# Expert 14's weighted rows added in memory like the others'; only the last expert is placed by TensorE in the combination

## The chip, the cores and the metric

The kernel runs on one core of one Trainium2 chip. A core has TensorE for matrix products (PE in the profile), VectorE (DVE), ScalarE (ACT), GpSimd (POOL) and SyncE (SP), each with its own list of instructions that it works through in order, and 16 DMA engines that move data between the chip's large memory and the on-chip memories. SyncE issues most of the transfers; GpSimd issues those that gather or scatter rows by an index. Engines wait for each other on semaphores. The metric is device time in microseconds of one execution, the median of several.

## The reference, cut to what matters

The program is a trunk of two layers over 512 tokens of width 1024. Each layer has a token mixer and then a mixture of 16 gated experts, of which each token uses two. What this case is about is the end of a layer:

```python
x = _layernorm(DEEPNORM_ALPHA * x + mix, ln1_g[l], ln1_b[l])
ffn = _hier_moe(x, ...)                      # sum over a token's two experts, weighted
x = _layernorm(DEEPNORM_ALPHA * x + ffn, ln2_g[l], ln2_b[l])

# inside _hier_moe, for all experts e:
h = silu(x @ w_gate[e]) * (x @ w_up[e]) * combine[..., e]
return einsum('bsef,efd->bsd', h, w_down)
```

The kernel divides by ALPHA ahead of a norm, so that it adds the experts' rows to x itself; the norm's epsilon is divided to match.

## The kernel before, in words

The 512 tokens stand as four tiles of 128 rows. After the first norm of a layer the four tiles are written twice to memory: to `x1d`, from which the experts gather their tokens, and to `acc`, to which the experts add their results (`keep`, line 1807). An expert has a block of up to 96 tokens. Its steps (class `Expert`) are: a selection matrix of 0 and 1 (`hot`), the row numbers from it (`index`), a gather of the rows from `x1d` (line 1446, GpSimd), transposes and a split of each operand into a high and a low part so that products keep float32's precision (`x`, `split`), the gate and up products (`up`), the activation (`act`), transposes of the hidden block (`hidden`) and the down product in two parts (`down`).

What then happens to the 96 result rows depends on the expert. For experts 0 to 13, `out` lets ScalarE scale them by the token's weight into a tile in two halves, and GpSimd issues one DMA that adds the 96 rows to the rows of `acc` that the index names (line 1598, a scatter with addition). For experts 14 and 15 nothing goes to memory. `place_t` turns the expert's selection matrix round by four small matmuls and a copy by ScalarE (`oht`), `y` leaves the scaled rows on the chip as a high part (ScalarE) and a low part (VectorE), and in the combination TensorE multiplies the turned selection with them, which places the rows in the tile's 128 rows.

The order of an expert's steps is written out (`ORDER`, line 59; loop at line 1962), with steps of neighbouring experts between each other; the results of expert e-1 leave within the turn of expert e, so those of expert 14 in the turn of expert 15. The loop pins the order of all but the last two turns, and a scheduler orders the rest by its own costs.

Behind the experts stands a loop for tokens beyond 96 of an expert (lines 1983 to 2039). Its count is read from a tile by every engine. With this case's inputs the count is 0 and the body is skipped, but the program counts semaphores as if it had run: on the skipping path each engine raises its own count by the number of the body's instructions, and GpSimd raises the counts of the body's DMAs, with one instruction behind waits for all counts of earlier software DMAs (`INC_SWDGE_SEM` in the profile, an `ISA` row in the order).

Then comes the combination (from line 2041). `load_x(acc)` loads the four tiles of `acc`; the combination's steps stand in `COMB0` for the first layer and `COMB1` for the second. For tile i, `F` is the first group of matmuls into two banks, `p` places the last expert's rows on top, `a` takes the sum out of the banks, `s`, `g`, `v`, `f` are the second norm. For tile 0 (`ACCD`) VectorE adds the banks to the loaded rows; for tiles 1 to 3 the loaded rows are added by TensorE, by a float32 product with the identity matrix ("identity matmul" below), and ScalarE takes the sum out together with its row sums. In the first layer the steps `w0` to `w3` split the first input weights of the next layer between them, and the transposes of the finished tiles open the next layer; in the second layer the finished tiles go to the output.

Of the kernel before, what the change touches and what calls it, by code (L numbers as in the profile page):

```python
# [25 lines left out]
E = 16  # L26
# [15 lines left out]
ACCD = (0,)  # L42
FL = 3
BLK = 96
# [142 lines left out]
class Buf:  # L187
# [4 lines left out]
    def free(self):  # L192
        assert self.live
        self.live = False
        self.pool.put(self)
# [17 lines left out]
def tile_trunk(ctx: ExitStack, tc: tile.TileContext, ins, out, dbg=None, depth=DEPTH):  # L213
# [22 lines left out]
    V, A, G, T = Pinned(nc.vector, "V"), Pinned(nc.scalar, "A"), nc.gpsimd, Pinned(nc.tensor, "T")  # L236
# [119 lines left out]
    ident = const.tile([128, 128], F32, name="ident")  # L356
# [202 lines left out]
    for l in range(depth):  # L559
# [1042 lines left out]
        def make(e):  # L1602
            def load_gu(t, q):
                load(t, ins["w_gu"], ((l * E + e) * 4 + q) * 128 * 1024, [[1024, 128], [1, 1024]])

            def load_dn(t, f):
                load(t, ins["expert_w_down"], ((l * E + e) * FE + f * 128) * D, [[D, 128], [1, D]])

            return Expert(load_gu, load_dn, e >= E - 2, e, e == 0)

        ex = [make(e) for e in range(E)]
# [18 lines left out]
        xr = load_x(ins["x"] if l == 0 else x2d)  # L1630
# [59 lines left out]
        for a, q in enumerate(order):  # L1690
            w = wo_split(raws[0][a], a)
# [124 lines left out]
        for c in WSEQ.split():  # L1816
            if c[0] == "Z":
                i = int(c[1])
# [21 lines left out]
            t = tiles[int(c[1])]  # L1840
# [14 lines left out]
        for _ in range(NU):  # L1855
            m, n = todo.pop(0)
# [61 lines left out]
        def all_experts():  # L1918
# [14 lines left out]
            for e in range(E):  # L1933
                if e == HE:
                    held[0] = None
                pin[0] = PIN0 <= e < E - PIN1
                a = ex[e]
                b, c, d = (ex[e + n] if e + n < E else None for n in (1, 2, RA))
                z = ex[e - 1] if e else None
                steps = {  # L1940
                    "act": a.act,
                    "out": (z.out if e < E - 1 else z.y) if z else None,
                    "hid": a.hidden,
                    "d0": lambda: a.down(0), "d1": lambda: a.down(1),
                    "sd0": lambda: a.split(4), "sd1": lambda: a.split(5),
                    "place": a.place_t if e >= E - 2 else None,
                }
                if e == E - 1:
                    steps["d0"] = steps["d1"] = None
# [26 lines left out]
        with tc.issue_after(kins.ins), tc.issue_after(tiles[NT - 1].cp.ins):  # L1976
            (first_w, first_w2), fr, fr2 = all_experts()
# [6 lines left out]
        with tc.If(rv > 0), tc.For_i(0, rv, 1):  # L1984
# [43 lines left out]
            m = Expert(load_gu, load_dn)  # L2028
# [13 lines left out]

        ln2 = load_ln(2)
        xr = load_x(acc)
        last = ex[E - 2:]

        def place(pz, i, m, first=False, final=False):
            t = m.oht[:BLK, i * 128:(i + 1) * 128]
            for hf, p in enumerate(pz):
                w = slice(hf * 512, hf * 512 + 512)  # L2050
                T.matmul(p.ap, t, m.yh[:BLK, w], start=first, stop=False, skip_group_check=True)
                T.matmul(p.ap, t, m.yl[:BLK, w], start=False, stop=final, skip_group_check=True)

        def first_places(i):
            pz = [(P4 if i > 1 else P5).get() for _ in range(2)]
            place(pz, i, last[0], first=True)
            if i not in ACCD:
                for hf, p in enumerate(pz):
                    T.matmul(p.ap, ident, xr[i][:, hf * 512:hf * 512 + 512], start=False, stop=False,
                             skip_group_check=True)  # L2060
            return pz

        class Norm:

# [8 lines left out]
            def place(self):  # L2073
                if self.pz is None:
                    self.first()
                place(self.pz, self.i, last[1], final=True)

            def sum(self):
                z = xr[self.i]
# [62 lines left out]
                first_w2[i] = (first_w2[i] or []) + win_split(fr2[i][q:q + 1], 0, 256, True)  # L2142
                free(fr2[i][q])

        last[1].down(0)
        last[1].down(1)
        norms = [Norm(i) for i in range(NT)]
        steps = {"y": last[1].y}
        for i in range(NT):
            n = norms[i]  # L2150
            for c, f in (("F", n.first), ("p", n.place), ("a", n.sum), ("s", n.square), ("g", n.scale),
# [3 lines left out]
            pin[0] = CPIN and c not in ("y", "w0", "w1", "w2", "w3")  # L2155
            steps[c]()
        pin[0] = False
        for m in last:
            free(m.oht, m.yh, m.yl)
        for n in range(NS, NS + KD):  # L2160
            pool.whole.remove(n)
        free(ln2)
# [67 lines left out]
```

## Time and profile before

| what | value |
|---|---|
| three runs | 1066.09, 1066.67, 1069.11 us; median 1066.67 |
| profiled execution | 1070.26 us, its span 1067.8 us |
| TensorE's granted clock, mean | 0.974 |
| busy share PE / DVE / ACT / POOL | 93% / 78% / 60% / 25% |
| scatters with addition | 28, 14 per layer |

The span is the time from the first to the last instruction; a share is the busy time over it. The first layer's combination lies at about 512 to 545 us, the second layer's at about 1040 to 1068 us, the end of the program. Times in all views are counted from the span's start.

### The profile page before, as it was taken

How to read it: one execution, taken by the hardware profiler on the slowest of the kernel's cores; microseconds unless marked ns; L12 is line 12 of the kernel's file. 1: busy time of each engine (PE TensorE's matmuls, PEld its weight loads, DVE VectorE, ACT ScalarE, POOL GpSimd, SP SyncE). 2: the span in 40 equal slices, each digit the busy share in tenths (PEclk: the TensorE clock that was granted, in tenths of full speed). 3: DMA queues.
4: the chain of work that ended last, by engine and by line, in shares of the span. 5: the costliest groups of instructions: out<-in, count | busy, mean ns of one | idle time of the engine just before them, and what ended most of it. 6: DMA issues, size and time to landing. Idle time of an engine off the chain costs nothing. (4 is left out here: it accounts for less than half of the span.)

```text
span 1067.8 us, 15553 instructions
## 1 busy us (share of the span) xinstructions
PE 996.5 (93%) x5310; PEld 739.2 (69%) x5310; DVE 836.0 (78%) x1832; ACT 644.6 (60%) x1182; POOL 267.2 (25%) x232
## 2 busy tenths in 40 slices
PE   6999999988998999999999999999799989999995
PEld 6876788555687666666598768876466876666653
DVE  8995557787749799999969955577876498999996
ACT  5565646555524588888646564466464347778874
POOL 1000002223003255565100000022220123556652
PEclk9999989998999899999999998999999989999998
DMA  7211100132656889996532120011347477999933
GB/s 305 69 45 45 40 21 21 35 126 99 234 198 218 282 288 345 335 324 213 204 139 70 40 69 1 21 40 41 118 138 246 168 275 264 311 339 337 308 94 155
DMA packets 51795, 176.76 MB, mean 166 GB/s; under 512 B 8169, under 2 KB 8681, under 8 KB 51712
## 3 DMA queue, kind: packets, MB, share of 16 engines
q1 hardware_dynamic: 45216, 160.42, 42.2%
q0 software_dynamic: 6496, 15.31, 6.0%
q8 instruction: 42, 0.69, 0.3%
q14 instruction: 41, 0.34, 0.1%
HBM read 159.61 MB, written 23.59 MB: 172 GB/s over the span
## 5 line engine op out<-in xcount | busy, mean ns | idle before, releaser
L230 PE MATMUL b<-xt,s 128*128 128x512 f32 (+3 forms) x1484 | 327.1, 367 | 13.8 <-ACT s L230 8.6
L230 PE MATMUL b<-s,s 128*128 128x512 f32 (+7 forms) x1308 | 324.7, 404 | 14.0 <-ACT s L230 7.1
L230 PEld LDWEIGHTS b<-xt,s 128*128 128x128 f32 (+2 forms) x1484 | 234.0, 183 | 80.3 <-issue 11.5
L230 DVE TENSOR_TENSOR s<-s,s 128x1024 fp32r<-128x1024 f32 (+8 forms) x254 | 247.6, 1000 | 50.5 <-ACT s L230 41.7
L230 PEld LDWEIGHTS b<-s,s 128*128 128x128 f32 (+3 forms) x1308 | 185.0, 173 | 99.7 <-DVE s L230 22.6
L230 ACT ACTIVATE s<-b 128x512 f32<-128x512 f32 (+8 forms) x282 | 135.0, 496 | 191.2 <-PE b L230 182.3
L230 ACT ACTIVATE s<-s 128x1024 fp32r<-128x1024 f32 (+5 forms) x219 | 191.6, 910 | 85.1 <-DVE s L230 31.8
L230 PE MATMUL b<-s,xt 128*128 128x256 f32 (+2 forms) x944 | 209.1, 362 | 0.4 <-POOL s L1523 0.4
L230 PEld LDWEIGHTS b<-s,xt 128*128 128x128 f32 (+1 forms) x944 | 150.6, 192 | 34.7 <-issue 4.8
L230 DVE TENSOR_TENSOR xt<-s,xt 128x1024 fp32r<-128x1024 f32 (+1 forms) x106 | 118.3, 1122 | 13.8 <-ACT xt L230 13.7
L230 ACT ACTIVATE xt<-s 128x1024 fp32r<-128x1024 f32 (+1 forms) x107 | 110.4, 1042 | 26.1 <-PE b L230 17.7
L230 PE MATMUL b<-ident,s 128*128 128x128 f32 (+3 forms) x736 | 107.4, 273 | 18.6 <-POOL s L1338 7.7
L230 PEld LDWEIGHTS b<-ident,s 128*128 128x128 f32 (+3 forms) x736 | 81.5, 153 | 53.3 <-ACT s L230 13.9
L1598 POOL DMA_INDIRECT acc<-s,slx x28 | 55.3, 1976 | 99.3 <-ACT s L230 79.4
L230 ACT ACTIVATE s<-b,mx,qsc 128x512 f32<-128x512 f32 x64 | 49.7, 782 | 25.5 <-DVE mx L230 25.1
L1338 POOL TENSOR_SCALAR s<-s,sums 128x512 f32<-128x512 f32 x48 | 37.6, 788 | 105.7 <-DVE sums L230 93.6
L1094 POOL MEMSET s<- 128x780 f32 x4 | 3.0, 756 | 219.9 <-DVE s L230 186.3
L230 DVE TENSOR_REDUCE mx<-b 128x1 f32<-128x512 f32 x64 | 43.2, 686 | 18.3 <-PE b L230 17.9
L1446 POOL DMA_INDIRECT s<-x1d,slx x30 | 40.5, 1351 | 57.4 <-PE b L230 23.0
L230 DVE TENSOR_TENSOR s<-b,s 128x192 fp32r<-128x192 f32 (+3 forms) x92 | 46.9, 524 | 4.6 <-POOL s L1127 2.6
L230 PE MATMUL b<-xt 128*96 128x512 f32 x160 | 48.0, 406 | 1.4 <-DVE xt L230 1.4
L230 ACT ACTIVATE s<-b,slw 96x512 f32<-96x512 f32 (+1 forms) x60 | 39.1, 682 | 14.9 <-PE b L230 8.3
(254 smaller groups left out, 983.9 us busy)
## 6 DMA issues: line engine op xcount, KB each, us to landing
s<-in_w_gu_dram SPq DMA_DIRECT2D x128, 512.0 KB
s<-in_expert_w_down_dram SPq DMA_DIRECT2D x64, 512.0 KB
s<-in_w_inp_dram SPq DMA_DIRECT2D x36, 512.0 KB
s<-in_w_outp_dram SPq DMA_DIRECT2D x16, 512.0 KB
x1d<-s SPq DMA_DIRECT2D x8, 512.0 KB
acc<-s SPq DMA_DIRECT2D x8, 512.0 KB
s<-acc SPq DMA_DIRECT2D x8, 512.0 KB
s<-in_x_t_dram SPq DMA_DIRECT2D x4, 512.0 KB
```

Source lines behind the costliest of these rows:

```text
L230: r = f(*a, **kw)
L1094: G.memset(cb.ap, 0.0)
L1338: (V if hd in NORMV else G).tensor_scalar(P.ap, P.ap, sums, 0.0, op0=OP.mult, op1=OP.add)
L1446: self.ga = G.indirect_dma_start(out=self.xg[:BLK], out_offset=None, in_=x1d[0:128 * n, :], in_offset=bass.IndirectOffsetOnAxis(ap=ix[:BLK ...
L1598: G.indirect_dma_start(out=acc[:, :], out_offset=bass.IndirectOffsetOnAxis(ap=self.ix[:BLK, 0:1], axis=0), in_=yt[:BLK], in_offset=None, b ...
```

## The change

Expert 14 now leaves like experts 0 to 13: ScalarE scales its rows into a tile, and GpSimd adds them to `acc` by a scatter, in the turn of expert 15. Its `place_t` and `y` are gone, and with them its part of the combination. `F` keeps only the identity matmuls (none for tile 0), and `p` places expert 15's rows alone.

```diff
-                    "out": (z.out if e < E - 1 else z.y) if z else None,
+                    "out": z.out if z else None,
...
-                    "place": a.place_t if e >= E - 2 else None,
+                    "place": a.place_t if e == E - 1 else None,
...
-        last = ex[E - 2:]
-
-        def place(pz, i, m, first=False, final=False):
-            t = m.oht[:BLK, i * 128:(i + 1) * 128]
+        last = ex[E - 1]
+
+        def first_places(i):
+            pz = [(P4 if i > 1 else P5).get() for _ in range(2)]
+            if i not in ACCD:
+                for hf, p in enumerate(pz):
+                    T.matmul(p.ap, ident, xr[i][:, hf * 512:hf * 512 + 512], start=True, stop=False,
+                             skip_group_check=True)
+            return pz
+
+        def place(pz, i):
+            t = last.oht[:BLK, i * 128:(i + 1) * 128]
             for hf, p in enumerate(pz):
                 w = slice(hf * 512, hf * 512 + 512)
-                T.matmul(p.ap, t, m.yh[:BLK, w], start=first, stop=False, skip_group_check=True)
-                T.matmul(p.ap, t, m.yl[:BLK, w], start=False, stop=final, skip_group_check=True)
-
-        def first_places(i):
-            pz = [(P4 if i > 1 else P5).get() for _ in range(2)]
-            place(pz, i, last[0], first=True)
-            if i not in ACCD:
-                for hf, p in enumerate(pz):
-                    T.matmul(p.ap, ident, xr[i][:, hf * 512:hf * 512 + 512], start=False, stop=False,
-                             skip_group_check=True)
-            return pz
+                T.matmul(p.ap, t, last.yh[:BLK, w], start=i in ACCD, stop=False, skip_group_check=True)
+                T.matmul(p.ap, t, last.yl[:BLK, w], start=False, stop=True, skip_group_check=True)
...
-                place(self.pz, self.i, last[1], final=True)
+                place(self.pz, self.i)
...
-        last[1].down(0)
-        last[1].down(1)
+        last.down(0)
+        last.down(1)
...
-        steps = {"y": last[1].y}
+        steps = {"y": last.y}
```

On GpSimd, in the first layer, this is what stands behind expert 13's scatter and ahead of the loop's count (`nblk`), before; `xt` and `s` are buffers, `slx` the row numbers, and the brackets name the semaphores waited for (`DMASW` those of GpSimd's own DMAs):

```order
L1598 DMA acc<-s_677_4794,slx_4404 512x1024 [waits DMASW4_49,DMASW3_49,Activation_49]
L1523 TENSOR_TENSOR xt<-s_621_4467,xt 128x512 [waits DVE_49,DMAHW5_49,PE_49,Activation_49]
L1523 TENSOR_TENSOR xt<-s_605_4371,xt 128x512 [waits DVE_49,DMAHW1_49,PE_49,Activation_49]
L1523 TENSOR_TENSOR xt<-s_625_4481,xt 128x512 [waits DMAHW7_49,Activation_49,Pool_49]
L1983 TENSOR_LOAD nblk_3194 [waits DVE_49]
L1984 COMPARE_AND_BRANCH x2
```

And the same place of the changed kernel, with the semaphore instruction of a path around the loop's body as its last row:

```order
L1598 DMA acc<-s_677_4794,slx_4404 512x1024 [waits DMASW4_49,DMASW3_49,Activation_49]
L1523 TENSOR_TENSOR xt<-s_621_4467,xt 128x512 [waits DVE_49,DMAHW5_49,PE_49,Activation_49]
L1523 TENSOR_TENSOR xt<-s_605_4371,xt 128x512 [waits DVE_49,DMAHW1_49,PE_49,Activation_49]
L1523 TENSOR_TENSOR xt<-s_625_4481,xt 128x512 [waits DMAHW7_49,Activation_49,Pool_49]
L1598 DMA acc<-s_679_4839,slx_4512 512x1024 [waits DMASW4_49,Activation_49]
L1983 TENSOR_LOAD nblk_3194 [waits DVE_49]
L1984 COMPARE_AND_BRANCH x2
L1984 ISA [waits DMASW4_49,DMASW5_49,DMASW3_49,DMASW6_49,DMASW2_49,DMASW7_49,DMASW1_49,DMASW0_49]
```

The new scatter stands between the last weight split and the loop, ahead of the instruction that waits for all eight counts. On SyncE, behind the loop, the first load of `acc` waits for the software DMA count 5 in the changed kernel, where it was count 4; in both it is the value that the count has after the loop:

```order
L277 DMA s_724_5067<-acc 128x1024 [waits DMASW5_49,DMAHW7_49,DVE_49,PE_49]
L277 DMA s_725_5069<-acc 128x1024 [waits DMAHW0_49,Activation_49]
L277 DMA s_726_5071<-acc 128x1024 [waits DMAHW1_49,DVE_49]
L277 DMA s_727_5073<-acc 128x1024 [waits DMAHW2_49,DVE_49,Pool_49]
L277 DMA s_785_5600<-in_w_inp_dram 128x1024 [waits DMAHW3_49,Activation_49]
```

On ScalarE, in the first layer's combination, before: `s_742` to `s_750` and `s_789` are splits of the next layer's input weights, `xt<-b` are the high parts of expert 15's rows, `s_725` is the sum of tile 1 taken out of its banks.

```order
L230 ACTIVATE s_742_5152<-s_673_4772 128x1024
L230 ACTIVATE s_744_5156<-s_674_4774 128x1024
L230 ACTIVATE xt<-b_72,slw_4622 96x512
L230 ACTIVATE xt<-b_71,slw_4622 96x512
L230 ACTIVATE s_748_5182<-s_675_4776 128x1024
L230 ACTIVATE s_750_5186<-s_676_4778 128x1024
L230 ACTIVATE s_725_5073,ac_5121<-b_75 128x512
L230 ACTIVATE s_725_5073,ac_5121<-b_73 128x512
L230 ACTIVATE s_789_5628<-s_785_5620 128x1024
```

And of the changed kernel:

```order
L230 ACTIVATE s_742_5140<-s_673_4772 128x1024
L230 ACTIVATE s_744_5144<-s_674_4774 128x1024
L230 ACTIVATE xt<-b_71,slw_4622 96x512
L230 ACTIVATE s_748_5166<-s_675_4776 128x1024
L230 ACTIVATE s_750_5170<-s_676_4778 128x1024
L230 ACTIVATE s_789_5608<-s_785_5600 128x1024
L230 ACTIVATE s_725_5069,ac_5109<-b_74 128x512
L230 ACTIVATE s_725_5069,ac_5109<-b_75 128x512
```

One half of expert 15's rows has moved ahead of the loop, and the split of `s_785`, which the load behind the four of `acc` brings, has moved ahead of tile 1's sum.

## Rows read from the trace of the kernel before

**Rows 1.** Chain that ended last, 1036 to 1068 us: start, length, engine and tile.
```profile
1040.85 11.27 PE b L230 x40
...
1062.11 1.28 DVE s L230
```

**Rows 2.** TensorE's groups by shape, 1042.9 to 1057 us: expert 14's placement.
```profile
L230 PE MATMUL b<-s,s 96*128 96x512 f32 x16 | 4.4, 396 | 0.0
```

**Rows 3.** Scatters of line 1598: who waited, all landings; landing in 500 to 512 us.
```profile
  POOL acc L1598: 3.9, 1
...
DMA to landing us min/median/max: 5.6/8.9/10.3
...
DMA to landing us min/median/max: 5.6/5.6/5.6
```

**Rows 4.** Time line, first combination: start, length, instruction, [idle before <-what ended it].
```profile
504.62 1.43 POOL L1598 DMA_INDIRECT acc<-s,slx  x1 [2.26 <-DVE xt L230]
...
510.60 0.33 SPq L277 DMA_DIRECT2D s<-in_ln_g_dram  x1
510.71 1.52 POOL L1523 TENSOR_TENSOR xt<-s,xt 128x512 fp32r<-128x512 f32 x1 [1.45 <-DVE s L230]
...
511.53 1.38 ACT L230 ACTIVATE s<-b,slw 96x512 fp32r<-96x512 f32 x2 [0.31 <-PE b L230]
512.56 3.50 SPq L277 DMA_DIRECT2D s<-acc  x4
...
520.15 1.98 PE L230 MATMUL b<-s,ident 128*128 128x512 f32 x4 [0.65 <-DMA s<-acc]
...
523.63 0.60 ACT L230 ACTIVATE s<-b 128x512 f32<-128x512 f32 x1 [3.31 <-PE b L230]
...
524.78 1.06 ACT L230 ACTIVATE s<-s 128x1024 fp32r<-128x1024 f32 x1
...
537.87 7.87 PE L230 MATMUL b<-xt,s 128*128 128x256 f32 x65
...
545.47 1.34 PEld L230 LDWEIGHTS b<-ident,s 128*128 128x128 f32 x12
```

**Rows 5.** Queue records of the skipped loop on GpSimd, ns, first and second layer.
```profile
L1984 POOLq INC_SWDGE_SEM  x1: 756/756/756, 511.8 to 511.8; - x1
...
L1984 POOLq INC_SWDGE_SEM  x1: 1322/1322/1322, 1038.5 to 1038.5; - x1
```

**Rows 6.** Time line, second combination.
```profile
1028.09 1.39 ACT L230 ACTIVATE s<-b,slw 96x512 f32<-96x512 f32 x2 [0.64 <-PE b L230]
...
1029.76 1.78 POOL L1598 DMA_INDIRECT acc<-s,slx  x1 [1.75 <-ACT s L230]
...
1037.37 1.79 POOL L1523 TENSOR_TENSOR xt<-s,xt 128x512 fp32r<-128x512 f32 x1 [3.27 <-ACT xt L230]
...
1038.27 1.38 ACT L230 ACTIVATE s<-b,slw 96x512 fp32r<-96x512 f32 x2 [0.32 <-PE b L230]
...
1039.92 1.84 SPq L277 DMA_DIRECT2D s<-acc  x4
...
1046.24 1.88 PE L230 MATMUL b<-s,ident 128*128 128x512 f32 x4
...
1048.62 0.60 ACT L230 ACTIVATE s<-b 128x512 f32<-128x512 f32 x1 [0.56 <-PE b L230]
```

**Rows 7.** Busy time by engine (us), PEclk, DMA share and GB/s, one full microsecond.
```profile
1042.00:1043.00 1.00, 1.00 (x6) 0.67 (x5) 0.00 (x0) 0.29 (x1) 0.00 (x0) 1.00 1.08 414
```

**Rows 8.** The same view: length, PE, PEld, DVE, ACT, POOL busy, then PEclk, DMA.
```profile
762.70:769.50 6.80, 2.30 (x10) 1.39 (x9) 5.37 (x15) 5.45 (x10) 2.01 (x2) 1.00 0.29 98
769.50:776.30 6.80, 5.31 (x15) 2.92 (x16) 5.52 (x13) 2.62 (x4) 2.68 (x3) 0.50 0.00 0
865.20:872.00 6.80, 4.18 (x41) 3.87 (x40) 6.51 (x27) 4.24 (x7) 2.67 (x2) 1.00 0.53 167
872.00:878.80 6.80, 6.67 (x28) 5.80 (x29) 5.24 (x24) 2.54 (x5) 1.47 (x2) 0.50 0.95 324
```

More of the change, by code (lines that the diff above doesn't have):

```diff
@@ L2157, in tile_trunk @@
         pin[0] = False
-        for m in last:
-            free(m.oht, m.yh, m.yl)
+        free(last.oht, last.yh, last.yl)
         for n in range(NS, NS + KD):
```

## The prediction, as put on record

> **What bounds the kernel now.** I read the views in this order: the chain that ended last, the time line of the two combinations, the queue records of the loop behind the experts, the scatters, and the granted clock of stretches. In the second combination the chain runs through TensorE for 11.27 us, and then through VectorE and ScalarE to the last normalisation at 1062.11 us [rows 1]. TensorE is what the placement loads: 16 matmuls of expert 14's rows take 4.4 us there [rows 2], four of them per tile in front of that tile's identity matmul. So a look at the busy share alone says that the change takes work off the chain. What decides is another chain, that ends just ahead of the combination: the last scatter, GpSimd's semaphore instruction behind the skipped loop, the four loads of `acc`, the first identity matmul.
>
> In the kernel before, that other chain has room. The scatter of expert 13 leaves GpSimd at 504.62 us in the first layer and its data are in memory 5.6 us later, at 510.2 [rows 3, 4]; GpSimd raises the counts of the loop's DMAs from 511.8 to 512.56 [rows 5], and SyncE starts the loads of `acc` at 512.56 [rows 4]. So it was GpSimd's arrival at the loop that released the loads, not the scatter. In the second layer the same instruction runs from 1038.5 to 1039.82 [rows 5], and the loads start at 1039.92 [rows 6], though expert 13's scatter had left at 1029.76. The first layer's combination already waits a little for the loads: TensorE's first identity matmul has 0.65 us of idle time ended by the DMA of `acc` [rows 4]. In the second layer it starts at 1046.24 with no such wait [rows 6].
>
> **What the change removes.** Per layer: 4 matmuls that transpose expert 14's selection, ScalarE's copy of it, VectorE's two residues of 14's rows (ScalarE's two scalings stay, they only write elsewhere), and the 16 placement matmuls [rows 2]. The first three stand ahead of the loop, where the chain to come starts at ScalarE's scalings, which wait for the weight splits of the last experts and not for these; I cost them at nothing, at most 0.5 us gained per layer. The placement matmuls were at most 4.4 us per layer [rows 2]. They are no gain while TensorE waits for `acc` longer than it worked on them.
>
> **What it adds: one scatter, ahead of the loads.** Its source is ready when ScalarE's second scaling ends. First layer: 511.53 + 1.38 = 512.91 [rows 4]; second: 1038.27 + 1.38 = 1039.65 [rows 6]. GpSimd starts 0.28 us behind (1028.09 + 1.39 = 1029.48, the scatter at 1029.76) [rows 6]; its own split before it is over by then (512.23 and 1039.16) [rows 4, 6]. So the scatters start at 513.19 and 1039.93. From start to landed I take 5.6 us, the one scatter with nothing issued behind it; all scatters with a landing in the trace lie between 5.6 and 10.3, median 8.9 [rows 3], but those run beside weight loads. Landed: 518.8 and 1045.5.
>
> GpSimd then stands at the loop: the order shows that its semaphore instruction waits for every DMA count, the new scatter's too, and the first load of `acc` waits for a count that this instruction raises. It takes 0.76 to 1.32 us [rows 5], 1.04 in the middle, and SyncE follows 0.1 later. Loads of `acc`: 519.9 instead of 512.56, and 1046.7 instead of 1039.92, some 7 us late. Behind the waiting load on SyncE stand the other three and the input weights of the next layer; behind GpSimd's instruction nothing that is due. ScalarE's second weight split in the first layer waits for a raised count as well, and expert 15's second half stands behind it; that is over by 522, ahead of the rows of `acc`.
>
> From the first load to TensorE's first identity matmul (tile 1): 520.15 - 512.56 = 7.6 us in the first layer [rows 4], with the two 0.5 MB loads of the norm's gain and bias in front; at the 414 GB/s of a full stretch [rows 7] they take 2.5 us, which leaves about 5.0. The second layer bounds it by 1046.24 - 1039.92 = 6.3 [rows 6]. With 5.0: 524.9 and 1051.7, which is 4.8 and 5.5 us late.
>
> **Second layer.** All later steps follow tile 1's rows, and from tile 1 on the chain is VectorE's and ScalarE's, which the change leaves alone [rows 1]. So +5.5, and the clock: TensorE now stands idle some 7 us before the identity matmul. In the rows, after it worked 2.30 us of a 6.8 us stretch the next one was granted 0.50, after 4.18 us as well, from 1.00 before each [rows 8]; that is 1.2 in place of 2.4 GHz. From the identity matmul to tile 1's sum on ScalarE were 2.38 us (1046.24 to 1048.62) [rows 6], so at half speed all through it is 2.4 more; the low level may end midway, and I take 1.6. Sum +7.1.
>
> A page speaks against the change here. The Trainium skill, "TensorE: Matmul & The Clock Gate", section "What's actually happening", has it that the throttled state is the default and that activity releases it. The rows above agree with it. Without that rule the second layer would stand at +5.5 and the sum below 1.6 lower.
>
> **First layer.** The order puts the split of the first loaded input weight ahead of tile 1's sum on ScalarE; before it stood behind. Its load is the fifth in the queue. Three loads after tile 1's rows at 1.27 us each (0.52 MB at 414 GB/s) it is there at 528.7, and 1.06 us of split [rows 4] end at 529.8. TensorE alone would let tile 1's sum begin at 524.9 + 3.48 (523.63 - 520.15) [rows 4] = 528.4, at the low clock some 1.6 later, 530.0. Both say 530: tile 1's sum moves from 523.63 to 530.0, +6.4. VectorE's scaling of tile 0 stands behind tile 1's mean, and tile 0's and 1's transposes feed the next layer. Slack is not to be seen behind it: VectorE is through with tile 3 just as TensorE comes to its transposes at 545.47 [rows 4].
>
> **Sum.** 6.4 + 7.1 = 13.5 us. The profiled execution took 1070.26 us, 2.5 of it outside its span of 1067.8, and becomes 1083.8. It was 3.6 us above the median of the runs, 1066.67; so the median goes to 1080.2. Bounds: low, the semaphore instruction takes 0.76, tile 1's rows come 4.4 us after the issue (the middle between the 6.3 above and the 2.5 that two tiles need at 414 GB/s), and the clock stays: +4.6 in the second layer and, with the weight split, +5.3 in the first, 9.9 together. High, the scatter lands after 8.9: 3.3 more in each layer.
>
> **Rivals.**
> 1. The clock stays at 1.00 and the next layer's weights are there in time: 4.8 + 5.5 = +10.3, 1077.0. For it: the rows of the clock show what went before, not how much idle time it takes; against it: 7 us idle is more than the 4.5 of [rows 8]. Chance 0.2.
> 2. The scatter needs what most need, 8.9 us: +13.5 + 6.6 = 1086.8. For it: the median [rows 3]; against it: weight loads run beside those, and here only the norm's two loads. Chance 0.12.
> 3. The first layer's delay is absorbed, because the next layer starts on weights and gates as well: +7.1 and about 1, 1074.8. Against it: TensorE's 7.87 us of the next projection, from 537.87, run right up to its wait for tile 3 [rows 4]. Chance 0.08, a quarter of it that the second layer is absorbed too and nothing moves.
> 4. The other side, faster: the loads go out in time and TensorE's 4.4 us per layer come off the chain, 1066.67 - 8.8 = 1057.9. That needs the first tiles' rows at about 1045 and 519, so loads that start no later than now, so a scatter that is landed within a few tenths of the moment its source is ready, or loads that need not wait for it. [rows 1, 2] speak for it, [rows 3] and the wait on the raised count against. Chance 0.04.
> The Trainium skill, "DMA: Bandwidth & Descriptors", section "Two DMAs through the same engine are not ordered", says that a dependent DMA has to wait for the first one's completion semaphore. By it rival 4 has no way out through queue order; GpSimd waited 3.9 us for a scatter before the next one [rows 3], which agrees.
>
> **How the numbers follow.** Forecast 0.56, rivals 0.2, 0.12, 0.08, 0.04. Likeliest 1080.2. The range from 1074 to 1087 takes in the forecast with its bounds, rivals 1 to 3, and leaves out rival 4 and the longest scatters. Some 0.3% (3.2 us) is what a measurement of this kernel tells from no change: slower 0.94, same 0.02, faster 0.04.
>
> **What would show it.** In the changed profile: 30 scatters; expert 14's starts within 0.5 us of ScalarE's second scaling; GpSimd's semaphore instruction ends only after it has landed; the loads of `acc` follow within 0.2 us; TensorE idle for 6 to 8 us ahead of the first identity matmul in each layer, its idle time ended by the DMA of `acc`; a granted clock of 0.50 right there; the split of the next layer's weight ahead of tile 1's sum, waiting for its DMA. Wrong it would be if the identity matmul began no later, counted from the end of ScalarE's second scaling, than 8.6 us (first layer, now 7.2) or 7.5 us (second, now 6.6).

## The result, and the profile after

| kernel | median (executions) | ratio to the kernel before, 95% interval |
|---|---|---|
| before | 1066.38 us (4) | |
| changed | 1080.79 us (4) | 1.0144 [1.0106, 1.0182] |
| changed, measured again later | 1079.05 us (5), before beside it 1063.62 (19) | 1.0157 [1.0136, 1.0177] |

The change costs 14.4 us by the first measurement and 15.4 by the second. The prediction had 1080.2 and 13.5. The profiled execution took 1080.08 us, its span 1078.3.

In the page, the group of the scatters now has 30 in place of 28:

```profile
L1598 POOL DMA_INDIRECT acc<-s,slx x30 | 58.9, 1965 | 98.1 <-ACT s L230 84.4
```

The time line of the first combination in the changed kernel (start, length, engine and instruction, idle time and what ended it), to be held against [rows 4]:

```profile
507.53 1.38 ACT L230 ACTIVATE s<-b,slw 96x512 f32<-96x512 f32 x2 [0.31 <-PE b L230]
...
509.18 1.41 POOL L1598 DMA_INDIRECT acc<-s,slx  x1 [0.76 <-DVE xt L230]
...
515.78 2.03 SPq L277 DMA_DIRECT2D s<-acc  x4
...
520.55 3.66 PE L230 MATMUL b<-s,ident 128*128 128x512 f32 x4 [5.37 <-DMA s<-acc]
...
525.45 1.06 ACT L230 ACTIVATE s<-s 128x1024 fp32r<-128x1024 f32 x1 [6.18 <-DVE s L230]
...
526.41 0.58 ACT L230 ACTIVATE s<-b 128x512 f32<-128x512 f32 x1
...
549.95 1.34 PEld L230 LDWEIGHTS b<-ident,s 128*128 128x128 f32 x12
```

And of the second, against [rows 6] and the last row of [rows 1]:

```profile
1040.88 1.38 ACT L230 ACTIVATE s<-b,slw 96x512 f32<-96x512 f32 x2
...
1042.61 1.42 POOL L1598 DMA_INDIRECT acc<-s,slx  x1 [0.15 <-ACT s L230]
...
1049.44 1.75 SPq L277 DMA_DIRECT2D s<-acc  x4
...
1054.07 3.78 PE L230 MATMUL b<-s,ident 128*128 128x512 f32 x4 [2.69 <-DMA s<-acc]
...
1058.74 0.60 ACT L230 ACTIVATE s<-b 128x512 f32<-128x512 f32 x1 [2.76 <-PE b L230]
...
1072.47 1.29 DVE L230 SCALAR_TENSOR_TENSOR s<-s,nr,s 128x1024 f32<-128x1024 f32 x1
```

One reading must be made first. Absolute times of two executions can't be subtracted here: expert 14's scaling comes 4.0 us earlier than before in the first layer (507.53 for 511.53) and 2.6 later in the second, and the first difference has arisen ahead of the changed place, in code that is the same: it is 2.5 us at 324 us, behind the token mixer, and 3.7 at 375, among the first experts. So I count every step from the end of ScalarE's second scaling of expert 14 in the same layer (508.91 and 1042.26 us here, 512.91 and 1039.65 before). The loads of acc then start 6.87 us behind it in the first layer, where they started 0.35 ahead of it, and 7.18 us in the second, where it was 0.27. The scatter lies between: it starts 0.27 and 0.35 us after the scaling, and lands 5.4 and 5.1 us later, by the trace's view of each scatter (first layer, then second):

```profile
DMA to landing us min/median/max: 5.4/5.4/5.4
...
DMA to landing us min/median/max: 5.1/5.1/5.1
```

GpSimd's counting stands behind the landing, in both layers. This is the view of the skipped loop's line on GpSimd (number, then minimum, median and maximum in ns, first and last start), against [rows 5]:

```profile
L1984 POOLq INC_SWDGE_SEM  x2: 776/1069/1362, 514.9 to 1048.0; - x2
```

The third thing to see is the clock. The view of stretches (from and to, length, TensorE's busy time, PEclk, DMA share, GB/s) of the changed kernel:

```profile
517.10:523.90 6.80, 3.35 (x5) 0.50 0.99 383
534.20:537.60 3.40, 3.40 (x17) 0.50 0.45 183
1053.00:1059.80 6.80, 5.73 (x9) 0.50 0.46 177
```

TensorE was idle 5.37 and 2.69 us ahead of its identity matmuls, and runs them at the lower level, 1.2 GHz: 3.66 and 3.78 us in place of 1.98 and 1.88 [rows 4, 6]. In the second layer it still worked on expert 15's down product and on tile 0's rows until 1051.39, so that only the end of its wait is idle time.

### The profile page after: what moved, and what is told of

It is laid out like the page before. It is cut to its first block, busy times and chain, and to the rows that moved or that the text cites. A ratio compares the mean times of both kernels' runs of the same rounds, so it can differ in the third digit from the quotient of the medians.

```text
span 1078.3 us, 15476 instructions
## 1 busy us (share of the span) xinstructions
PE 990.6 (92%) x5270; PEld 730.3 (68%) x5270; DVE 834.6 (77%) x1828; ACT 643.9 (60%) x1180; POOL 271.2 (25%) x234
## 5 line engine op out<-in xcount | busy, mean ns | idle before, releaser
L230 PE MATMUL b<-xt,s 128*128 128x512 f32 (+3 forms) x1484 | 330.8, 370 | 18.0 <-ACT s L230 8.3
L230 PE MATMUL b<-s,s 128*128 128x512 f32 (+8 forms) x1276 | 316.0, 404 | 14.1 <-ACT s L230 6.8
L230 PEld LDWEIGHTS b<-xt,s 128*128 128x128 f32 (+2 forms) x1484 | 236.3, 185 | 87.0 <-issue 15.7
L230 PEld LDWEIGHTS b<-s,s 128*128 128x128 f32 (+2 forms) x1276 | 178.9, 172 | 98.0 <-DVE s L230 23.4
L230 ACT ACTIVATE s<-b 128x512 f32<-128x512 f32 (+7 forms) x280 | 134.2, 496 | 183.4 <-PE b L230 174.4
L230 PE MATMUL b<-s,xt 128*128 128x256 f32 (+2 forms) x944 | 203.5, 354 | 0.4 <-POOL s L1523 0.4
L230 PEld LDWEIGHTS b<-s,xt 128*128 128x128 f32 (+1 forms) x944 | 144.8, 184 | 34.3 <-issue 4.8
L230 DVE TENSOR_TENSOR xt<-s,xt 128x1024 fp32r<-128x1024 f32 (+1 forms) x106 | 118.2, 1122 | 14.6 <-ACT xt L230 14.6
L1598 POOL DMA_INDIRECT acc<-s,slx x30 | 58.9, 1965 | 98.1 <-ACT s L230 84.4
L230 ACT ACTIVATE s<-b,slw 96x512 f32<-96x512 f32 x60 | 39.0, 682 | 14.7 <-PE b L230 8.1
```

The lines of the kernel that those rows point to most:

```text
L230: r = f(*a, **kw)
L1598: G.indirect_dma_start(out=acc[:, :], out_offset=bass.IndirectOffsetOnAxis(ap=self.ix[:BLK, 0:1], axis=0), in_=yt[:BLK], in_offset=None, b ...
```

## The experiments

All ran with a profile and were timed against runs of the kernel before on the same chip, whose medians lay between 1063.62 and 1065.39 us. The profiled executions lie from 4 us below to 7 us above the medians of their kernels; so the traces say where a step stands, and the medians what a change costs. The table gives the time, and three points of each combination, in us from the end of ScalarE's scaling of expert 14: the identity matmul's start (that of tile 1's rows, not of a filling product), the start of tile 1's sum, and the end of the last normalisation of tile 3. Where a combination is that of the kernel before, the points differ by up to 0.9 us between executions in the first layer, and by less than 0.1 in the second.

| kernel | median | ratio to before [interval] | first layer | second layer |
|---|---|---|---|---|
| before | | | 7.2, 10.7, 32.4 | 6.6, 9.0, 23.7 |
| changed | 1080.79 | 1.0144 [1.0106, 1.0182] | 11.6, 17.5, 39.1 | 11.8, 16.5, 31.5 |
| changed, again | 1079.05 | 1.0157 [1.0136, 1.0177] | 11.1, 16.8, 37.9 | 11.9, 16.3, 31.0 |
| first layer only | 1072.64 | 1.0082 [1.0054, 1.0110] | 11.3, 17.5, 39.0 | not changed: 6.6, 9.0, 23.8 |
| second layer only | 1071.97 | 1.0074 [1.0045, 1.0103] | not changed: 7.0, 10.5, 32.1 | 11.6, 16.3, 31.3 |
| no scatter | 1067.92 | 1.0032 [1.0006, 1.0057] | 6.8, 13.1, 34.1 | 7.1, 9.6, 24.4 |
| no scatter, filled | 1066.23 | 1.0010 [0.9993, 1.0028] | 6.9, 10.3, 31.6 | 7.0, 9.5, 24.2 |
| filled | 1075.43 | 1.0104 [1.0078, 1.0130] | 11.0, 14.4, 36.7 | 12.1, 14.6, 29.3 |
| one filling product | 1079.86 | 1.0142 [1.0114, 1.0171] | 11.2, 16.2, 37.4 | 11.6, 16.3, 31.3 |
| 32 rows | 1078.42 | 1.0132 [1.0103, 1.0161] | 10.6, 15.7, 37.1 | 10.9, 15.4, 30.2 |
| no count | 1080.81 | 1.0141 [1.0105, 1.0176] | 14.4, 20.4, 41.6 | 10.3, 14.4, 29.2 |
| before, no count | 1066.92 | 1.0025 [1.0004, 1.0047] | 11.3, 14.6, 36.3 | 6.1, 8.6, 23.3 |
| three placed | 1067.18 | 1.0043 [1.0027, 1.0059] | 8.0, 11.3, 32.8 | 8.1, 10.5, 25.4 |
| before, wide sums | 1063.88 | 0.9996 [0.9974, 1.0017] | not changed: 7.9, 11.4, 33.0 | not changed: 6.6, 9.0, 23.8 |

**One layer at a time.**

```diff
-                    "out": z.out if z else None,
+                    "out": (z.out if e < E - 1 or l in NEW else z.y) if z else None,
-                    "place": a.place_t if e == E - 1 else None,
+                    "place": a.place_t if e >= (E - 1 if l in NEW else E - 2) else None,
```

with NEW the first layer or the second, and the combination following it.

> The change in the first layer alone; the second layer places expert 14's rows by TensorE as before. Theory (the scatter's landing holds up the loads of acc, layer by layer): the delay of this layer alone, by the offsets of the two traces (tile 3's transposes 8.5 us later, counted from ScalarE's second scaling of expert 14) and scaled to the measured 14.4 us of both layers, 7.5 us: 1074 us, between 1071.5 and 1076. By the prediction's own term (6.4 us) 1072.8. Rival (the next layer absorbs most of a late start, and the second layer carries nearly all of the 14.4 us): below 1069.

> The change in the second layer alone; the first places expert 14's rows by TensorE as before. Theory: 7 us (the trace of the changed kernel has the last normalisation 7.75 us later, counted from ScalarE's second scaling of expert 14; the prediction's term was 7.1): 1073.4 us, between 1071 and 1075.5, with nothing moved ahead of the second combination. Rival (the first layer carries nearly all): below 1069. The two kernels' differences from the kernel before should add up to 14.4 us within 2.

Measured: 1072.64 and 1071.97 us beside 1064.81, so 7.8 and 7.2 us. They add up to 15.0, which is the change's whole loss (14.4 and 15.4). In the execution with the first layer alone the second combination has the times of before. Both rivals, that one layer carries nearly all, are out.

**The scatter left out.** Expert 14's rows are scaled and dropped.

```diff
+                if self.e == E - 2:
+                    yt.free()
+                    return
                 G.indirect_dma_start(out=acc[:, :], ...
```

> The changed kernel without expert 14's scatter: its rows are scaled and then dropped, so that they are missing in the output; nothing places them. All that the change removes is gone, and the wait that it adds is not there. Theory (the wait is the whole loss, and the removed work was covered): the loads of acc start when GpSimd reaches the loop, as before, TensorE's first identity matmul still waits for them, and the time is the kernel before's or up to 3 us below it: 1063.5 to 1067. Rival (the removed placement came off the chain, and the change gains it back): 4.4 us per layer, 1057.6. Rival (the loss comes from the other order of the instructions and not from the scatter): near 1080.

Measured: 1067.92 us, some 12 us below the changed kernel and 3.1 above the kernel before. So the scatter carries some 12 us of the loss, and the other order of the instructions at most the 3.1 that are left; but with the removed work gone and the scatter gone too, nothing is gained. The rival of 1057.6 is out. The expectation missed too, by about 1 us on the other side, and its time line says why (first combination, as above):

```profile
513.32 1.37 ACT L230 ACTIVATE s<-b,slw 96x512 f32<-96x512 f32 x2 [0.31 <-PE b L230]
514.40 2.03 SPq L277 DMA_DIRECT2D s<-acc  x4
...
521.50 3.78 PE L230 MATMUL b<-s,ident 128*128 128x512 f32 x4 [2.74 <-DMA s<-acc]
524.29 3.93 PE L230 MATMUL b<-xt,s 96*128 96x512 f32 x8
527.80 0.60 ACT L230 ACTIVATE s<-b 128x512 f32<-128x512 f32 x1 [6.37 <-PE b L230]
```

The loads start ahead of the scaling's end again, and the identity matmul is no later than before (6.8 us for 7.2). But the eight placement matmuls that stood in front of it in the kernel before are missing, TensorE waits 2.74 us, and then runs at half clock: 3.78 and 3.93 us in place of 1.98 and 2.44. Tile 1's sum comes 2.4 us later than before.

**The same with TensorE kept at work.** Products of the norm's gain and the identity matrix, overwritten by what follows:

```diff
+            if i == 1:
+                for k in range((3, 1)[l]):
+                    T.matmul(pz[k % 2].ap, ident, ln2[0][:, 0:512], start=True, stop=True, ...)
             if i not in ACCD:
```

> The kernel without expert 14's scatter (its rows are missing in the output), which ran 3 us slower than the kernel before, with the same filling matmuls: 3 in the first layer, 1 in the second. Its trace had TensorE idle for 2.74 us ahead of the first layer's identity matmul, where the kernel before places expert 14's rows for 2.0 us, and then the identity matmuls took 3.78 us in place of 1.98. Theory (the removed placement had kept TensorE at full clock while it waited): clock 1.00 there, tile 1's sum some 2.8 us earlier in the first layer, and the time 2 to 3 us below the kernel without filling, within 1.5 us of the kernel before. Rival (the 3 us come from elsewhere, the order on ScalarE or the granted clock of other stages): no difference to the kernel without filling.

Measured: 1066.23 us, 1.7 below the kernel without filling; the two intervals overlap, so by the times alone the difference is not shown. The time line shows it at its place:

```profile
515.05 2.74 PE L230 MATMUL b<-s,ident 128*128 128x512 f32 x6
...
517.98 1.98 PE L230 MATMUL b<-s,ident 128*128 128x512 f32 x4 [0.20 <-DMA s<-acc]
...
521.40 0.60 ACT L230 ACTIVATE s<-b 128x512 f32<-128x512 f32 x1 [3.53 <-PE b L230]
```

The rows of acc come as late as without filling (6.9 us behind the scaling for 6.8), and from the identity matmul to tile 1's sum it is 3.4 us in place of 6.3. So TensorE's placement of expert 14 was not only hidden: while it waited for acc it kept the clock up. Filled, the kernel without scatter stands where the kernel before does, which is what the removed work is worth in time: nothing that can be measured.

**The changed kernel filled**, with 5 and 3 such products in the two layers.

> The changed kernel with products of the norm's gain and the identity matrix, whose results are overwritten, ahead of TensorE's first identity matmul: 5 in the first layer (about 5 us of work, in place of its idle time before the rows of acc), 3 in the second. Theory (part of the loss is TensorE's clock at half after the idle time; the identity and placement matmuls of tiles 0 and 1 took 6.4 us there in place of 4.4 in the first layer, 6.5 in place of 3.4 in the second): granted clock 1.00 at the identity matmul, tile 1's sum 1.5 to 2.5 us earlier after it, and the time 2 to 4 us below the changed kernel's: 1077 to 1079 us. Rival (VectorE and ScalarE set the end behind the rows of acc whatever TensorE does): the same as the changed kernel's, or 1 us more.

Measured: 1075.43 us; 1.0104 [1.0078, 1.0130] against 1.0157 [1.0136, 1.0177] for the changed kernel, so 0.53%, 5.6 us, less (0.40%, 4.3 us, against the first measurement, 1.0144 [1.0106, 1.0182], whose interval overlaps). That is more than the 2 to 4 us expected. Clock and first combination:

```profile
521.00:525.00 4.00, 3.94 (x13) 1.00 1.01 401
1052.00:1056.00 4.00, 3.93 (x11) 1.00 0.57 227
```

```profile
516.18 4.45 PE L230 MATMUL b<-s,ident 128*128 128x512 f32 x10
...
521.05 1.98 PE L230 MATMUL b<-s,ident 128*128 128x512 f32 x4 [0.42 <-DMA s<-acc]
...
524.48 0.60 ACT L230 ACTIVATE s<-b 128x512 f32<-128x512 f32 x1 [4.44 <-PE b L230]
...
1052.07 1.98 PE L230 MATMUL b<-s,ident 128*128 128x512 f32 x4 [1.61 <-DMA s<-acc]
...
1054.55 0.60 ACT L230 ACTIVATE s<-b 128x512 f32<-128x512 f32 x1 [0.52 <-PE b L230]
```

The identity matmul starts no earlier by more than its spread (11.0 and 12.1 us), but tile 1's sum 2.4 to 3.1 us earlier in the first layer and 1.7 to 1.9 in the second. The rival, that VectorE and ScalarE set the end whatever TensorE does, is out. What is left is in the main the bare wait: the identity matmul stands 3.7 and 5.5 us later than before.

**One filling product.** In the kernel with 5 and 3 the scheduler had also put the split of the next layer's weight behind tile 1's sum on ScalarE. One product in the first layer, (1, 0) in the edit above, gives the same order without the filling.

> The changed kernel with one filling product in the first layer (about 1 us of work) and none in the second. It has the same order on ScalarE as the kernel with 5 and 3 filling products (the split of the next layer's weight stands behind tile 1's sum, where the changed kernel has it ahead), but leaves TensorE idle for most of its wait for acc. It tells apart what the filling gained in the first layer. Theory (the clock): TensorE's clock is at half at the identity matmul as in the changed kernel, the order alone is worth what ScalarE's split ends later than TensorE's banks, 0.4 to 0.9 us: about 1078.5 us, 1 below the changed kernel (1079 to 1080.8). Rival (the order of ScalarE): all that the filling gained in the first layer, 2 to 3 us, comes with the one product: 1076.5. If one product already keeps the clock up, the granted clock in the trace will say so, and this run tells nothing of the order.

Measured: 1079.86 us, no gain that can be measured. The clock was at half for a shorter while than in the changed kernel, 3.4 us, so this run is a test of the order only in part:

```profile
519.50:522.90 3.40, 3.40 (x7) 0.51 1.03 417
```

```profile
518.74 3.03 PE L230 MATMUL b<-s,ident 128*128 128x512 f32 x4 [4.05 <-DMA s<-acc]
...
523.80 0.60 ACT L230 ACTIVATE s<-b 128x512 f32<-128x512 f32 x1 [6.11 <-PE b L230]
```

From the identity matmul to tile 1's sum it is 5.1 us; 5.7 and 5.9 in the two executions of the changed kernel, 3.4 filled. At most 0.6 to 0.8 us are the order's, and some of that is the clock's.

**A shorter scatter**, 32 of the 96 rows.

```diff
+                n = 32 if self.e == E - 2 else BLK
-                                     in_=yt[:BLK], in_offset=None, ...
+                                     in_=yt[:n], in_offset=None, ...
```

> The changed kernel with 32 in place of 96 rows in expert 14's scatter; the other 64 rows are missing in the output. Theory (the path runs through the scatter's landing): whatever the scatter gets shorter from start to landing, the count, the loads and the identity matmul come as much earlier in both layers; if the landing has a fixed part of about 3.5 us and the rest goes with the rows, 1.3 us per layer, 2.6 in all: 1078 us. If all of the 5.2 to 5.4 us went with the rows, 3.6 per layer: 1073.5. Rival (the loads are held by something else than the landing): no difference.

Measured: 1078.42 us, against 1079.05 and 1080.79; the intervals overlap, so the time alone doesn't decide. The first layer's scatter, loads and identity matmul in the trace, and the scatter's landing:

```profile
509.74 1.31 POOL L1599 DMA_INDIRECT acc<-s,slx  x1 [0.76 <-DVE xt L230]
...
514.42 3.16 SPq L277 DMA_DIRECT2D s<-acc  x4
...
520.09 3.33 PE L230 MATMUL b<-s,ident 128*128 128x512 f32 x4 [4.35 <-DMA s<-acc]
...
DMA to landing us min/median/max: 3.5/3.5/3.5
```

The scatter lands after 3.5 us in place of 5.0 to 5.4, the loads start 1.5 to 1.9 us earlier (4.95 us behind the scaling for 6.45 and 6.87), and tile 1's sum 1.1 to 1.8. In the second layer the loads start 0.8 to 1.0 us earlier and the sum 0.9 to 1.1. With a third of the bytes the landing thus takes about two thirds of the time. In the second layer the identity matmul follows in full (0.9 to 1.0 us earlier). In the first it comes only 0.4 to 1.0 us earlier, since from the loads to it there are 5.7 us in place of 4.6 to 4.8; why was not found. The rival, that something else holds the loads, is out.

**The count taken out.** The loop's body, skipped with these inputs, becomes one small write by SyncE, so that GpSimd has no counts to raise.

```diff
         with tc.If(rv > 0), tc.For_i(0, rv, 1):
-            ind = small([128, 3, E], tag="ind", bufs=1)
...
-            m.out()
+            nc.sync.dma_start(dram(acc, 0, [[D, 128], [1, 1]]), bcur)
             V.tensor_scalar(bcur, bcur, 1.0, None, op0=OP.add)
```

> The changed kernel with another body in the loop for tokens beyond 96 of an expert, which these inputs skip: one small write to acc by SyncE in place of the body's expert, so that GpSimd has no DMAs in it whose counts it must raise, and SyncE's loads of acc wait for expert 14's scatter itself. Theory (scatter, then count, then load in a row): the loads start 0.1 to 0.3 us after the scatter has landed in place of 1.16 us (first layer) and 1.7 us (second), so both combinations come 0.9 and 1.4 us earlier: 1078.5 us, and the loss of the change is still 12 us. Rival (the count, not the scatter, is what costs: without it the loads need not wait): near 1066.

Measured: 1080.81 us, no gain, where 2.3 us were expected. The time line, first and second combination:

```profile
509.42 4.29 SPq L277 DMA_DIRECT2D s<-in_w_inp_dram  x2
...
512.21 2.43 POOL L1598 DMA_INDIRECT acc<-s,slx  x1 [0.54 <-DVE xt L230]
...
521.85 1.75 SPq L277 DMA_DIRECT2D s<-acc  x4
...
1047.46 1.41 POOL L1598 DMA_INDIRECT acc<-s,slx  x1 [0.16 <-ACT s L230]
...
1052.90 1.75 SPq L277 DMA_DIRECT2D s<-acc  x4
```

In the second layer it went as expected: the scatter lands after 5.4 us, at 1052.83, the loads start 0.07 later, and the end comes 1.8 to 2.3 us earlier than in the changed kernel. In the first layer the loads follow the landing as closely (0.06 us), but the scatter takes 9.6 us: with other instructions in the loop the scheduler issues weight loads of the next layer just ahead of it (that these make it long is argued, no run shows it alone). That costs what the other layer gains. So the loads wait for the scatter itself, and the count is 1.1 to 1.6 us on top. The two layers' numbers also show what the prediction's second rival would have looked like.

**The kernel before without the count.** The same edit in the kernel before.

> The kernel before, with the small body in the skipped loop, so that the loads of acc wait for expert 13's scatter itself and not for GpSimd's counts (tokens beyond 96 of an expert are left out, of which these inputs have none). In the kernel before both identity matmuls start within 0.3 us of the landing of tile 1's rows. Theory (the loads of acc set the start of both combinations, TensorE's placement only fills the time until then): loads earlier by 1 to 2 us, and the identity matmul as far as placing expert 14 allows: 0.5 to 2 us faster than the kernel before. Rival (TensorE's placement sets the start): the same as before.

Measured: 1066.92 us, 2.1 slower, so not the gain expected. In the first layer this kernel has another order (expert 15's steps come later, and the clock is at half at 517 us), and says nothing on the question. In the second:

```profile
1039.38 1.75 SPq L277 DMA_DIRECT2D s<-acc  x4
1042.37 1.38 ACT L230 ACTIVATE s<-b,slw 96x512 fp32r<-96x512 f32 x2 [0.31 <-PE b L230]
...
1049.88 1.88 PE L230 MATMUL b<-s,ident 128*128 128x512 f32 x4
```

The loads start 4.4 us ahead of the scaling's end in place of 0.3 behind it, and the identity matmul comes 0.5 us earlier. In the second layer of the kernel before, loads and placement were thus in balance within half a microsecond: earlier loads alone gain next to nothing (the end comes 0.4 us earlier).

**Three experts placed**, a step in the other direction.

```diff
-                    "out": (z.out if e < E - 1 else z.y) if z else None,
+                    "out": (z.out if e < E - 2 else z.y) if z else None,
-        last = ex[E - 2:]
+        last = ex[E - 3:]
```

> A step in the other direction from the kernel before: expert 13 leaves by TensorE too, so that three experts are placed in the combination (16 more matmuls of 0.275 us per layer) and the last scatter is expert 12's. Theory (a scatter decides only when it lands behind GpSimd's arrival at the loop, which expert 13's did not in the kernel before; the placement of tiles 0 and 1 stands ahead of the first sum): the loads of acc start no earlier, tile 1's sum comes later by eight placement matmuls, 2.2 us, less the 0.65 us that TensorE waited in the first layer: 1.5 + 2.2, some 4 us slower than the kernel before, 1068.5, between 1066 and 1071. Rival (each expert less in memory gains): below 1064. Rival (all 32 matmuls on the path): 8.8 us slower, 1073.6.

Measured: 1067.18 us, 3.6 slower than the kernel before (4 expected). In the second layer:

```profile
1036.40 1.37 ACT L230 ACTIVATE s<-b,slw 96x512 fp32r<-96x512 f32 x2 [0.32 <-PE b L230]
1037.96 1.75 SPq L277 DMA_DIRECT2D s<-acc  x4
...
1045.89 1.88 PE L230 MATMUL b<-s,ident 128*128 128x512 f32 x4
```

The loads start no earlier (0.2 us behind the scaling), the identity matmul 1.5 us later, and the end 1.6. In the first layer the points move by 0.8 us at most, no more than between executions of the kernel before. Tile 1's sum thus comes 0.6 and 1.5 us later, where 1.5 and 2.2 were expected: the total was met, but some 1.5 us of it lie outside these points, and their place stays open. Two placed experts are the best of one, two and three.

**The clock in the token mixers.** The column sums in the mixers with 64 equal columns of ones in place of one, in the kernel before:

```diff
-                    T.matmul(p[:, g * NT + i:g * NT + i + 1], sq[...], ones[:, 0:1],
+                    T.matmul(p[:, (g * NT + i) * 64:(g * NT + i + 1) * 64], sq[...], ones[:, 0:64],
```

> The kernel before with one edit in its token mixers: the column sums that TensorE forms by a column of ones (128x1 products, 3.08 us of them at 132.4 us in the first layer, behind which the granted clock stood at half for 6.8 us, and again in the second layer at 660 us) are formed with 64 equal columns of ones in place of one; the result is read from the first. Theory (the clock falls behind stretches in which TensorE moves little, and that costs time where TensorE is the bound, as the filled runs show for the combination): no half clock behind 132 and 658 us; each of these stretches costs up to 2.7 us by the offsets between the traces with and without it, so 2 to 5 us faster than the kernel before: 1060 to 1063. Rival (the granted clock there has other reasons): same as before, or 1 us slower by the wider products.

Measured: 1063.88 us, no difference. The first row is of the kernel before, the two others of this one:

```profile
134.70:141.50 6.80, 6.80 (x32) 0.50 0.00 0
```

```profile
134.70:141.50 6.80, 6.75 (x54) 1.00 0.01 2
930.40:933.80 3.40, 3.40 (x14) 0.50 1.03 377
```

The low clock behind the sums is gone, in both layers, and the execution is 4.5 us ahead of the kernel before by 680 us. But the changed kernel's execution, with the sums as they were, has none at 134 us either, so it is not there in each execution; and that the wider sums are what removed it is not shown by one trace. This execution, the slowest of the twelve (1071.09 us), also gives the lead back, part of it at 930 us, where the clock falls in the midst of the experts. What it is that gives it back was not found.

**The changed kernel again.**

> The changed kernel once more, unchanged, on the same chip as the two others and with more executions, so that the experiments have a narrower figure to stand against. All theories: 1080.8 us, between 1078 and 1083, 13 to 17 us above the kernel before.

Measured: 1079.05 us, 15.4 above the kernel before, as expected. None of these kernels beats the kernel before by more than can be measured, and none of them points to one that would.

## Why the prediction was right, step by step

1. The chain from the scaling to the loads was right. The scatters start 0.27 and 0.35 us behind it (0.28 predicted), land after 5.4 and 5.1 us (5.6), the count takes 0.78 and 1.36 (1.04), and the loads of acc follow within 0.1. That the loads wait for the landing is shown by taking the scatter out, shortening it, and taking the count out.
2. From the loads to the identity matmul 4.8 and 4.6 us (5.0), so that it comes 4.4 and 5.2 us later than before (4.8 and 5.5).
3. "They are no gain while TensorE waits for acc longer than it worked on them": right that there was no gain, but the removal wasn't free, as the sum had it. Even with the loads in time, the missing placement let TensorE stand idle and the clock fall, 2.4 us up to tile 1's sum in the first layer (no scatter against before). Rival 4, faster by 8.8 us, would thus not have come even if the loads had.
4. The clock was the term that was mis-sized, and the idle time ahead of it was misread. The prediction had TensorE idle for 6 to 8 us ahead of the identity matmul in each layer; it was 5.37 and 2.69 us (4.79 and 3.62 in the second execution), and the clock fell even so. It took 1.6 us for the clock in the second layer, and in the first it let the clock disappear behind the weight split ("Both say 530"). In the second layer it measured 2.3 us (from the identity matmul to tile 1's sum 4.7 for 2.4), in the first 2.4 (5.9 for 3.5, with at most the 0.6 to 0.8 us of point 5 in it), and the filled kernel removed both. Filling took back 4.3 to 5.6 us of the whole, by the ratios. Since the wait came out 0.4 and 0.3 us shorter than predicted (point 2) and the clock (in the first layer with the split) 0.8 and 0.7 dearer, the two errors in part cancel in the sum; that part of the agreement is luck. By a rule of the Trainium skill, page "TensorE: Matmul & The Clock Gate", section "What's actually happening", the throttled state is the default and activity releases it; the filled runs agree, with 1.00 in place of 0.50 at the identity matmul.
5. The weight split ahead of tile 1's sum was there, and ends at 526.51 in the changed kernel, 0.1 us behind the start of the sum in the trace. That it waits for its DMA, as predicted, stands in the second execution's trace; in the first one's the wait is put down to VectorE. It weighs at most 0.6 to 0.8 us by the run with one filling product, since TensorE's banks were as late.
6. Tile 1's sum moved by 6.8 and 6.0 us in the two executions of the changed kernel in the first layer (6.4 predicted), and the last normalisation of the second by 7.8 and 7.3 (7.1). In the first layer that was not the end of it: tile 3's transposes start 41.0 us behind the scaling, for 32.6 before, 8.5 later. The prediction took TensorE's work there as run right up to tile 3 and moved it with the rest; but a second stretch at half clock, from 534.2, lies on the transposes of tile 0, which take 3.44 us for 2.02. The first two lines are of the changed kernel, the last of the kernel before:

```profile
533.85 1.23 DVE L230 TENSOR_TENSOR s<-s,s 128x1024 fp32r<-128x1024 f32 x1
533.86 3.44 PE L230 MATMUL b<-ident,s 128*128 128x128 f32 x16 [2.46 <-DVE nr L230]
```

```profile
531.44 2.02 PE L230 MATMUL b<-ident,s 128*128 128x128 f32 x16 [0.28 <-DVE nr L230]
```

The clock is not all of it. VectorE's part of a weight split (533.85) has moved between the last normalisations of tiles 0 and 1, which now start 3.7 us apart (532.43 and 536.11) for 2.55 before (530.02 and 532.57). From tile 1's sum to tile 3's transposes the changed kernel takes 23.6 us and the kernel before 22.0; the kernels without scatter and the one with one filling product have VectorE's new order and full clock there, and take 22.5 to 22.9, while the filled kernel takes 23.8 at full clock. So at most some 1.1 us of the rest are the low clock's; how it divides is argued from traces, not shown by a run. Timed alone, the first layer costs 7.8 us.
7. The sum of 13.5 stands against 14.4 and 15.4, inside its bounds. Rival 1, the clock staying up, was priced at +10.3; the filled kernel, which makes it come true, measures +10.6 by the medians. Rival 2's long scatter came up in the first layer of the run without the count, where weight loads ran beside it, as the argument against it said. Rival 3 is out by the runs of one layer.

## What to carry to other kernels

Work may be taken off an engine only after looking at what it waits for behind that work: here about half of the 4.4 us of placement matmuls of a layer stood ahead of the first identity matmul (2.02 us in the first layer), cost next to nothing there, and kept the clock up too; the other half was no gain either. Before a result is sent through memory, count the whole chain of its last part (scatter from start to landing, count, load, first use: some 12 us here from the scaling to the identity matmul) against what the consumer does meanwhile; what is produced last is best kept on the chip. And compare executions from a step that both share, not by absolute times.

## What the runs showed of the hardware that was not expected

- After 2.74 us of idle time TensorE ran the identity matmul of the first layer without scatter at half clock; after 4.05 us, with one filling product, the clock was at half for a shorter while. That cost 2.9 and 1.6 us up to tile 1's sum, against the filled kernels. Not each such wait did it: after 2.22 us, in the kernel before with wide sums, the same matmuls took 1.98 us, as at full clock.
- A scatter with addition of 96 rows took 5.0 to 5.6 us to land with little beside it and 9.6 with weight loads issued 2.8 us ahead of it, in one execution; of 32 rows 3.5.
- A product with 64 columns took about as long as one with a single column (275 for 250 ns, median). Behind the wide ones the granted clock was 1.00 in the one execution with a trace; behind the narrow ones it was 0.50 in the kernel before and 1.00 in the changed kernel.
